# Side jobs at half the density in the pair stage, the time steps' sums among them; attention's units split before their value products; 1.4 instead of 1.5 pieces of filler a scan step

## The chip, the cores and the metric

The kernel runs on one core of one Trainium2 chip, as one launch. A core has a matrix engine (TensorE, PE in the profile; PEld are its weight loads), a vector engine (VectorE, DVE), an activation engine (ScalarE, ACT), a general engine (GpSimd, POOL), a queue engine that issues most transfers (SyncE, SP), and 16 DMA engines. Each engine works through its own list of instructions in order; semaphores let one wait for another. The metric is the device time in microseconds (us); lower is better.

## The reference

One layer of a streaming encoder on 1024 prompt tokens and 64 tokens of a running stream (1088 in all here), width 1024, all in float32:

```python
xn = _rmsnorm(x, p['norm_mix_w'])
proj = xn @ p['w_in']
z, xbc, dt_raw, q, k, v, gate_ssm, gate_att = jnp.split(proj, ...)
xbc_c = jax.nn.silu(causal_dwconv(conv_past, xbc))
dt = jax.nn.softplus(dt_raw + p['ssm_dt_bias'])      # the time steps
y_ssm, ssm_new = _ssd_scan(xs, dt, -exp(p['ssm_a_log']), bm, cm, ...)
q = _partial_rope(_rmsnorm(q, p['q_norm_w']), q_pos)
k = _partial_rope(_rmsnorm(k, p['k_norm_w']), q_pos)
o = _diff_attention(q, k_all, v_all, q_pos, k_pos, lam)
o = _rmsnorm(o, p['subln_w']) * (1.0 - lambda_init)
mix = sigmoid(gate_ssm) * (y_ssm @ w_branch_ssm) + sigmoid(gate_att) * (o @ w_branch_attn)
x = x + mix @ p['w_out']
x = x + ConvFFN(_rmsnorm(x, p['norm_ffn_w']))
```

Attention has 8 heads of two components each (the second's probabilities are subtracted, weighted), in blocks of 128 queries; the scan works on chunks with decays from running sums of dt times a constant per head.

## The kernel before

Each float32 operand is split into a high and a low part (`split`: ACT casts the high part, DVE subtracts), and a product is three matmuls of 128 x 128 weights with 272 columns (high-high, high-low, low-high). The stages, in order of time:

- **Values** (to about 152 us): `values(f, ...)` makes four groups of 256 columns of v, two of them with dt beside it. While `third` and `fourth` run, `rooted(k)` prepares the rows for the next stage on DVE and ACT, and after the tenth of their units `steps()` computes the time steps: some 20 vector instructions on 128 x 288, then sums over tokens on TensorE (L469, L472 and the nine of L482), whose results go to `nacum`, `decs`, `dtw` and to the scratch tensor `a_sc`, which the scan reads.
- **Pairs** (about 152 to 776 us): the projections q, k, z and the convolution inputs ("c"), 26 pairs of 2 x 128 columns, by a seven-product scheme. A pair is 14 groups (p, s) of 12 matmuls, in `pile` at L597; after each group ACT or DVE takes the result out of the bank (`u1`, `u2`, `pre`). The order of pairs is INPUT: 4 of q, 4 of k, 3 of z, then three times four of "c" and one of z. A "c" pair also has four convolutions of three vector instructions (L627). Beside the groups go side jobs, a generator `beside` advanced by `next(beside, None)`: `cached_keys`, `finishing("q")` and `finishing("k")`, which norm q and k, write k to the output and, at the end, rotate two of the eight row tiles in four parts (`turned`: L735 to L748). A side job loads in one part and works in the next (`in_turn`), and draws its row tiles from the rings "fx" (two) and "fc" (three), the latter shared with the convolutions.
- **Attention** (about 780 to 1244 us): per head nine blocks in ATT_ORDER. `attend` makes scores (L950, L951) and softmax, stops, and later does transposes (L979) and value products (L998); DEEP = 2 blocks lie between. When a head's last block is done, `head_out` norms its outputs (`o_t`, L1019 on DVE), transposes them (L1020) and stores them. Between blocks, `fill(ATT_STEPS)` issues pieces of a filler, projections of gates and z by `project` (L155 to L157, in 24 matmuls of 272 columns); a rate of 1 stands for 363 columns.
- **Scan** (about 1240 to 1690 us): 36 steps over chunks and groups with 12 turns between spans; at each of the 48 turns `fill(SCAN_STEPS)` issues filler, first what is left of the gates, then two of the three branch products. What remains is run behind the scan, and then the third branch product, which reads the scan's last rows back from DRAM (L205 casts them).
- **Output and feed-forward** (to the end).

The source order is not the order on the engines: a scheduler places every instruction on its engine's list by priority and by its own estimate of time. `tc.issue_after(x)` keeps what it encloses from being placed before instruction x; `seen[...]` holds the last instruction of a kind. `stat(w)` gives the one bank of its kind for small sums, `acc(w)` the next of seven banks.

Of the kernel before, what the change touches and what calls it, by code (L numbers as in the profile page):

```python
# [17 lines left out]
P = 128  # L18
# [50 lines left out]
SCAN_STEPS = 1.5  # L69
# [14 lines left out]
def hybrid_layer(ctx: ExitStack, tc: tile.TileContext, xT, xt, prm, cst, rope, wvd, win, wbs, wba, wout, wup, wdn,  # L84
# [360 lines left out]
    def steps():  # L445
        four = [raw_row(n) for n in ("da", "af")]
        da, e, t = (four[0][:, 288 * i : 288 * (i + 1)].rearrange("p (a b) -> p a b", b=32) for i in range(3))
        tail = raw_row("dt2")
        t2 = tail[:, :288].rearrange("p (a b) -> p a b", b=32)
        u = dtw  # L450
        act(e, u, AF.Abs)
        act(e, e, AF.Exp, scale=-1.0)
        V.tensor_scalar_add(t, e, 2.0)
        V.reciprocal(t, t)
        V.tensor_tensor(out=t, in0=t, in1=e, op=ALU.mult)
        V.tensor_tensor(out=t2, in0=t, in1=t, op=ALU.mult)
        V.tensor_scalar(e, t2, 1.0 / 17, None, ALU.mult)
        for n in (15, 13, 11, 9, 7, 5, 3):
            V.scalar_tensor_tensor(e, e, 1.0 / n, t2, ALU.add, ALU.mult)
        V.scalar_tensor_tensor(e, e, 1.0, t, ALU.add, ALU.mult)  # L460
        V.tensor_scalar_max(u, u, 0.0)
        V.scalar_tensor_tensor(dt_tok, e, 2.0, u, ALU.mult, ALU.add)
        an = tail[:, 288:320]
        act(an, par[:, O_AL : O_AL + 32], AF.Exp)
        V.scalar_tensor_tensor(da, dt_tok, -1.0, an.unsqueeze(1).to_broadcast([P, 9, 32]), ALU.mult, ALU.mult)
        V.memset(da[TS:, 8, :], 0.0)
        flat = lambda x: x.rearrange("p a b -> p (a b)")
        pa = acc(288)
        PE.matmul(pa, tri, flat(da), start=True, stop=True)  # L469
        V.tensor_scalar(flat(nacum), pa, -1.0, None, ALU.mult)  # L470
        pl = acc(288)
        PE.matmul(pl, ones, flat(da), start=True, stop=True)  # L472
        act(flat(decs), pl, AF.Exp)
        V.tensor_tensor(out=flat(dtw), in0=pl, in1=flat(nacum), op=ALU.add)
        act(dtw, dtw, AF.Exp)
        V.tensor_tensor(out=dtw, in0=dtw, in1=dt_tok, op=ALU.mult)
        af = four[1][:32]
        for c, w in WIDE:
            pf = acc(512)
            for i in range(c // P, -(-(c + w) // P)):  # L480
                n = min(P, T - i * P)
                PE.matmul(pf[:32, i * P - c : i * P - c + n], da[:n, i], tri[:n, :n], start=True, stop=True)  # L482
            V.tensor_copy(af[:, c : c + w], pf[:32, :w])
        load(out=a_sc[:8].rearrange("c h t -> h c t"), in_=af[:, :TP].rearrange("h (c t) -> h c t", t=P))
        load(out=a_sc[8, :, :TS], in_=af[:, TP:T])
# [98 lines left out]
    def in_pair(n):  # L584
# [5 lines left out]
        def pile(key, p, s, start):  # L590
# [3 lines left out]
            for k in range(4):  # L594
                c = slice(P * k, P * (k + 1))
                for i, (x, y) in enumerate(((0, 0), (0, 1), (1, 0))):
                    PE.matmul(ps, w[x][:, c], b[y][:, k], start=start and k == i == 0, stop=k == 3 and i == 2,  # L597
                              skip_group_check=not start)
# [84 lines left out]

    def in_turn(items):
# [12 lines left out]
    def finishing(kind):  # L697
# [6 lines left out]
        for c, w in WIDE:  # L704
            ps = stat(w)
            PE.matmul(ps, blk, rs[:, c : c + w], start=True, stop=True)
# [71 lines left out]

    early = [plain_left(0), plain_left(1)]
# [21 lines left out]
    for n in range(1, len(INPUT)):  # L801
        coming = in_parts(n + 1) if n + 1 < len(INPUT) else iter(())
        u = pairs[1] if n == 1 else begun_in(n)
        for at, (p, s) in enumerate(rest if n == 1 else [(p, s) for p in range(7) for s in range(2)]):
# [3 lines left out]
            if at % 2 == 0:  # L808
                next(beside, None)
# [62 lines left out]
    with (tc.tile_pool(name="ak", bufs=1) as ak, tc.tile_pool(name="at", bufs=1) as at,  # L872
# [209 lines left out]
        for f in late:  # L1082
            f()
# [704 lines left out]
```

## Time and profile before

| | |
|---|---|
| median of 3 runs | 2616.3 us (2616.27 to 2619.97) |
| the profiled execution | 2610.97 us; its span 2609.2 us |
| TensorE busy | 2419.7 us, 93% of the span, mean granted clock 0.968 |
| DVE, ACT, POOL busy | 1790.5, 1233.3, 738.4 us |
| TensorE busy, 400 to 500 us | 66.2 us of 100, granted clock 0.81 |
| TensorE busy, 800 to 1200 us | 86 to 92 us of 100, granted clock 0.90 to 0.93 |

A row of the waits names engine, tile and line, then the engine, tile and line that released it, the total, how often, and the longest. A row of stretches has the stretch, its length, then busy time and instructions of PE, PEld, DVE, ACT and POOL, the granted clock as a share of full speed, the mean busy share of the DMA engines, and GB/s. A row in order of time has start, length, engine, line, operation, output<-input, shapes and count, and in brackets the idle time before it with what ended it.

### The profile page before, as it was taken

How to read it: one execution, taken by the hardware profiler on the slowest of the kernel's cores; microseconds unless marked ns; L12 is line 12 of the kernel's file. 1: busy time of each engine (PE TensorE's matmuls, PEld its weight loads, DVE VectorE, ACT ScalarE, POOL GpSimd, SP SyncE). 2: the span in 40 equal slices, each digit the busy share in tenths (PEclk: the TensorE clock that was granted, in tenths of full speed). 3: DMA queues.
4: the chain of work that ended last, by engine and by line, in shares of the span. 5: the costliest groups of instructions: out<-in, count | busy, mean ns of one | idle time of the engine just before them, and what ended most of it. 6: DMA issues, size and time to landing. Idle time of an engine off the chain costs nothing.

```text
span 2609.2 us, 48402 instructions
## 1 busy us (share of the span) xinstructions
PE 2419.7 (93%) x18504; PEld 2324.4 (89%) x18504; DVE 1790.5 (69%) x3063; ACT 1233.3 (47%) x2613; POOL 738.4 (28%) x702
## 2 busy tenths in 40 slices
PE   9599998599998988889999999799999999998999
PEld 8599888599998878778878889799999999998999
DVE  4656776789885666664578766664897767778763
ACT  6244363345444555554576665433443333344441
POOL 0002223245420000000344433201245554545443
PEclk9799999799999988989999999999999999999999
DMA  7645657532246544532679785566323324348974
GB/s 247 216 159 191 226 164 249 168 113 101 101 138 205 159 144 142 163 114 75 221 267 307 264 292 171 158 188 208 114 87 109 143 75 178 114 157 253 228 200 88
DMA packets 282410, 449.72 MB, mean 172 GB/s; under 512 B 34937, under 2 KB 185602, under 8 KB 282178
## 3 DMA queue, kind: packets, MB, share of 16 engines
q1 hardware_dynamic: 274978, 433.54, 50.4%
q0 software_dynamic: 7200, 13.09, 3.2%
q8 instruction: 145, 2.38, 0.4%
q14 instruction: 87, 0.71, 0.1%
HBM read 294.03 MB, written 152.50 MB: 171 GB/s over the span
## 4 chain that ended last, share of the span: by engine, by line
PE 53%; DVE 10%; DMA 8%; ACT 5%; issue 3%; POOL 2%; SPq 1%; DVEq 0%; POOLq 0%; ACTq 0%
PE mx L1449 8%; PE mx L597 7%; PE mx L1607 4%; PE mm L155 4%; PE mm L157 4%; PE mm L156 4%; PE mm L1449 3%; PE po L998 3%; PE mm L597 3%; PE mm L1607 2%; PE mx L155 1%; PE mx L157 1%; PE mx L156 1%; PE sc L950 1%; DMA ht<-h_sc 1%
## 5 line engine op out<-in xcount | busy, mean ns | idle before, releaser
L155 PE MATMUL mm<-b,w_hi 128*128 128x272 f32 x1152 | 345.0, 300 | 18.9 <-ACT b L205 11.6
L157 PE MATMUL mm<-b,w_lo 128*128 128x272 f32 x1152 | 339.5, 295 | 2.6 <-DVE w_lo L149 2.4
L156 PE MATMUL mm<-b,w_hi 128*128 128x272 f32 x1152 | 339.9, 295 | 0.0
L155 PEld LDWEIGHTS mm<-b,w_hi 128*128 128x128 f32 x1152 | 220.8, 192 | 26.0 <-ACT b L205 13.3
L1128 POOL TENSOR_SCALAR_AFFINE_SELECT bc<-bc 128x1024 f32<-128x1024 f32 (+1 forms) x36 | 40.3, 1119 | 659.5 <-DMA start<-in_st_dram 506.1
L157 PEld LDWEIGHTS mm<-b,w_lo 128*128 128x128 f32 x1152 | 220.5, 191 | 6.4 <-DVE w_lo L149 4.5
L156 PEld LDWEIGHTS mm<-b,w_hi 128*128 128x128 f32 x1152 | 221.1, 192 | 4.2 <-issue 3.0
L405 DVE TENSOR_TENSOR wh<-w_f,wh 128x512 fp32r<-128x512 f32 (+1 forms) x174 | 173.6, 999 | 50.0 <-ACT wh L404 49.8
L524 POOL TENSOR_TENSOR ws<-w_f 128x512 f32<-128x512 f32 (+1 forms) x56 | 78.9, 1408 | 449.9 <-DMA q_r<-pre 186.6
L404 ACT CAST w_hi<-ws 128x512 fp32r<-128x512 f32 (+1 forms) x120 | 73.3, 611 | 170.0 <-PE mx L1449 74.6
L1449 PE MATMUL mx<-n,wh 128*128 128x272 f32 x1128 | 150.1, 288 | 1.9 <-ACT wh L404 1.1
L1449 PEld LDWEIGHTS mx<-n,wh 128*128 128x128 f32 x1128 | 144.5, 188 | 2.5 <-ACT wh L404 1.3
L1449 PE MATMUL mx<-m,w_hi 128*128 128x272 f32 x752 | 144.9, 290 | 1.2 <-DVE hb L1485 0.8
L964 ACT ACTIVATE p_t<-sc,mx 128x512 f32<-128x512 f32 (+5 forms) x144 | 106.2, 740 | 79.1 <-DVE mx L955 24.3
L597 PE MATMUL mx<-t,wh 128*128 128x272 f32 x936 | 129.8, 293 | 8.1 <-DVE u L668 8.1
L597 PE MATMUL mx<-t,w_hi 128*128 128x272 f32 x568 | 111.0, 291 | 24.0 <-ACT pre L677 24.0
L627 DVE SCALAR_TENSOR_TENSOR cc<-pre,par,cc 128x544 f32<-128x544 f32 (+1 forms) x144 | 131.4, 940 | 0.4
L597 PEld LDWEIGHTS mx<-t,wh 128*128 128x128 f32 x936 | 123.0, 191 | 9.7 <-DVE u L668 9.2
L404 ACT CAST wh<-w_f 128x512 fp32r<-128x512 f32 (+1 forms) x174 | 106.4, 615 | 49.5 <-issue 14.9
L597 PE MATMUL mx<-b,wh 128*128 128x272 f32 x864 | 118.6, 292 | 4.4 <-ACT u L666 4.4
L1466 POOL TENSOR_TENSOR hb<-hb,cc 128x544 f32<-128x544 f32 (+2 forms) x66 | 90.5, 1385 | 107.0 <-DVE hb L1487 49.4
L1449 PEld LDWEIGHTS mx<-m,w_hi 128*128 128x128 f32 x752 | 117.9, 188 | 2.5 <-DVE hb L1485 2.0
(445 smaller groups left out, 7408.1 us busy)
## 6 DMA issues: line engine op xcount, KB each, us to landing
w_f<-in_win_dram SPq DMA_DIRECT2D x78, 512.0 KB, 4.0
w_f<-in_wup_dram SPq DMA_DIRECT2D x45, 512.0 KB, 3.7
bc<-a_sc SPq DMA_DIRECT2D x32, 512.0 KB, 5.8
h_sc<-hb SPq DMA_DIRECT2D x44, 272.0 KB, 2.1
ht<-h_sc SPq DMA_DIRECT2D x22, 544.0 KB, 4.7
t_sc<-ht SPq DMA_DIRECT2D x22, 544.0 KB, 2.8
out_dram<-yq POOLq DMA_DIRECT2D x44, 272.0 KB, 6.0
g_sc<-gt SPq DMA_DIRECT2D x64, 136.0 KB, 2.4
```

The costliest lines, as they stand in the source:

```text
L155: PE.matmul(ps, a_hi, b_hi, start=i == 0, stop=False)
L156: PE.matmul(ps, a_hi, b_lo, start=False, stop=False)
L157: PE.matmul(ps, a_lo, b_hi, start=False, stop=i == n - 1)
L404: S.copy(hi, src)
L405: V.tensor_tensor(out=lo, in0=src, in1=hi, op=ALU.subtract)
L524: by.tensor_tensor(out=s1, in0=q21, in1=q22, op=ALU.add)
L597: PE.matmul(ps, w[x][:, c], b[y][:, k], start=start and k == i == 0, stop=k == 3 and i == 2, skip_group_check=not start)
L627: V.scalar_tensor_tensor(cc[:, :n], pre[:, i : i + n], cw(i), cc[:, :n], ALU.mult, ALU.add)
L964: act(p_t[:n, :nk], sc[c][:n, :nk], AF.Exp, bias=mx[:n, c : c + 1], accum_out=dst)
L1449: PE.matmul(ps, w[x][:, c], b[y][:, k], start=start and k == i == 0, stop=k == 3 and i == 2, skip_group_check=not start)
L1466: G.tensor_tensor(out=hb[h][:, o : o + n], in0=hb[h][:, o : o + n], in1=cc[:, d : d + n], op=ALU.mult)
L1607: PE.matmul(ps, w[y][:, c], b[z][:, k], start=start and k == j == 0, stop=k == n - 1 and j == 2, skip_group_check=not start)
```

## The change

Five edits:

1. `steps()` is a generator now, in eight parts, and runs as the first of the side jobs instead of between the value units. It draws its rows from the pair stage's rings and one tile of the ring "ss", its sums use `stat`, and `issue_after` puts them behind the latest product of the pair.
2. A side job's part comes after every fourth group instead of every second; `finishing("q")` and `finishing("k")` are both appended after the fourth pair, so that one follows the other. The sums within `finishing` are placed behind the latest product, too.
3. In attention, a unit stops a second time, between its transposes and its value products, and the filler is issued there instead of after the value products.
4. `head_out` is a generator: the nine scalings in its first part, one empty part, then its transposes in three parts, one part a block.
5. SCAN_STEPS is 1.4 instead of 1.5.

```diff
-SCAN_STEPS = 1.5
+SCAN_STEPS = 1.4
...
-    def steps():
-        four = [raw_row(n) for n in ("da", "af")]
...
-    for i, u in enumerate(chain(third, fourth)):
+    for u in chain(third, fourth):
         next(making, None)
-        if i == 9:
-            steps()
...
-                    PE.matmul(ps, w[x][:, c], b[y][:, k], ...)
+                    seen["mm"] = PE.matmul(ps, w[x][:, c], b[y][:, k], ...)
...
+    def steps():
+        flat = [four[:, 288 * i : 288 * (i + 1)] for i in range(3)] + [row("fx", "dt2")[:, :288]]
...
+        V.tensor_tensor(out=t2, in0=t, in1=t, op=ALU.mult)
+        yield
+        V.tensor_scalar(e, t2, 1.0 / 17, None, ALU.mult)
...
+        pa = stat(288)
+        with tc.issue_after(seen["mm"].ins):
+            PE.matmul(pa, tri, flat(da), start=True, stop=True)
+        V.tensor_scalar(flat(nacum), pa, -1.0, None, ALU.mult)
+        yield
...
+        for c, w in WIDE:
+            af = row("fc", "af")[:32, :w]
+            pf = stat(512)
...
+            yield
...
-    beside = cached_keys()
+    beside = chain(steps(), cached_keys())
...
-            if at % 2 == 0:
+            if at % 4 == 0:
                 next(beside, None)
...
-        if n in (3, 7):
-            beside = chain(beside, finishing("q" if n == 3 else "k"))
+        if n == 3:
+            beside = chain(beside, finishing("q"), finishing("k"))
...
                     V.tensor_copy(a4[:TS, :n], pt[:TS, :n])
+            yield
             po = pa.tile([P, 512], F32, name="po", tag="pt", bufs=2)
...
+            for i in range(9):
+                n = min(P, T - i * P)
+                V.scalar_tensor_tensor(o_t[:n, i], o_t[:n, i], rs[:n, i : i + 1], wsub[:n], ALU.mult, ALU.mult)
+            yield
+            yield
             for b0 in range(0, 9, 4):
...
-                    V.scalar_tensor_tensor(o_t[:n, i], o_t[:n, i], rs[:n, i : i + 1], wsub[:n], ALU.mult, ALU.mult)
                     PE.transpose(pt[:, (i - b0) * P : (i - b0) * P + n], o_t[:n, i], ident[:n, :n])
...
+                yield
...
                 unit, done = waiting.pop(0)
+                next(unit)
+                with tc.issue_after(seen["scores"].ins):
+                    fill(rate)
                 run(unit)
                 if done is not None:
-                    late.append(done)
+                    run(ended)
+                    ended = done()
...
-                while late:
-                    late.pop(0)()
+                next(ended, None)
...
-                settle(DEEP)
-                with tc.issue_after(seen["scores"].ins):
-                    fill(ATT_STEPS)
+                settle(DEEP, ATT_STEPS)
```

Where instructions stand now. First TensorE's list in the value stage, before: the steps' sums (L469, L472, L482; `da` is their operand) between two value units.

```order
L157 MATMUL mm<-b_906,xn_lo_102 128x256
L469 MATMUL mm<-da,con 128x288
L472 MATMUL mx<-da,con 128x288
L482 MATMUL mx<-con,da 32x128 x8
L482 MATMUL mx<-con,da 32x64
L155 MATMUL mx<-b_904,xn_hi_101 128x256
```

After, on TensorE in the pair stage (L553 are the products of a pair, L666 the first sum, whose operand lies in the tile `st`):

```order
L553 MATMUL mm<-b_1611,w_hi 128x272
L553 MATMUL mm<-b_1612,w_hi 128x272
L553 MATMUL mm<-b_1611,w_lo 128x272
L666 MATMUL st<-st,con 128x288
L553 MATMUL mm<-t_926,wh 128x272
```

The sums have moved from the value stage into the pair stage, between two groups, and the value units follow one another. Second, DVE's list where k is rotated, before (L741 to L748 are a rotation, L405 with `rt` its split; `rp` are cosines and sines):

```order
L741 SCALAR_TENSOR_TENSOR x<-x,par,ss 128x272 x2
L745 TENSOR_TENSOR rt<-x,rp 128x544
L741 SCALAR_TENSOR_TENSOR x<-x,par,ss 128x272 x2
L746 TENSOR_TENSOR x<-x,rp 128x544
L747 TENSOR_TENSOR x<-x,rt 128x272
L748 TENSOR_TENSOR x<-x,rt 128x272
L745 TENSOR_TENSOR rt<-x,rp 128x544
L746 TENSOR_TENSOR x<-x,rp 128x544
```

After, the same on DVE (L753 to L756 are L745 to L748 of before; L635 and L624 take a pair's results out of the banks, L583 is the convolution):

```order
L754 TENSOR_TENSOR x<-x,rp 128x544
L635 TENSOR_TENSOR pre<-mx,u_6318 128x272
L755 TENSOR_TENSOR x<-x,rt 128x272
L756 TENSOR_TENSOR x<-x,rt 128x272
L635 TENSOR_TENSOR pre<-mx,u_6318 128x272
L583 SCALAR_TENSOR_TENSOR cc<-pre,par,cc 128x547
L405 TENSOR_TENSOR w_lo<-ws_6356,w_hi 128x512
L405 TENSOR_TENSOR w_lo<-w_f,w_hi 128x512
L583 SCALAR_TENSOR_TENSOR cc<-pre,par,cc 128x547
L405 TENSOR_TENSOR x<-x,rt 128x544
```

Before, two rotations stood in each other, with nothing of a pair between; now the pair's own rows lie between a rotation's. Third, TensorE's list at the end of a head, before (L950 and L951 scores, L1020 the transposes of `head_out`, L979 those of a unit, L998 value products):

```order
L950 MATMUL sc<-kh_10044,q_10042 128x256
L951 MATMUL sc<-kl_10047,q_10042 128x256
L1020 MATMUL pt_10223<-con,o_t 128x128 x4
L1020 MATMUL pt_10238<-con,o_t 128x128 x4
L1020 MATMUL pt_10253<-con,o_t 128x64
L979 MATMUL pt<-con,p_t 128x128 x4
L950 MATMUL sc<-kh_10055,q_10061 128x512
```

After, around the second of the three pieces on TensorE (L1034 is L1020 of before, L988 is L979, L1008 is L998, L959 and L960 the scores; the first piece stands 35 rows earlier and the third 12 later):

```order
L959 MATMUL sc<-kh_9984,q_9982 128x128
L960 MATMUL sc<-kl_9987,q_9982 128x128
L1008 MATMUL po<-v_t,a_t 128x128
L1034 MATMUL pt_10356<-con,o_t 128x128 x4
L959 MATMUL sc<-kh_9995,q_10001 128x512
L960 MATMUL sc<-kl_9998,q_10001 128x512
L959 MATMUL sc<-kh_10004,q_10001 128x128
```

The nine transposes have been torn into three pieces with scores, value products and filler between them, and DVE's scalings for them stand ahead of the first.

More of the change, by code (lines that the diff above doesn't have):

```diff
@@ L705, in finishing @@
             ps = stat(w)
-            PE.matmul(ps, blk, rs[:, c : c + w], start=True, stop=True)
+            with tc.issue_after(seen["mm"].ins):
+                PE.matmul(ps, blk, rs[:, c : c + w], start=True, stop=True)
             t = [row("fx", "n1") for _ in range(2)]
@@ L777, in begun_in @@
         return u
+    four = row("ss", "st")
     early = [plain_left(0), plain_left(1)]
@@ L1026, in head_out @@
                     load(out=o_sc[D * u + P * h : D * u + P * (h + 1), b0 * P : b0 * P + w], in_=t.bitcast(F32))
+                yield
         fill(FIRST)
@@ L1081, in hybrid_layer @@
         settle(0)
-        for f in late:
-            f()
+        run(ended)
     with (tc.tile_pool(name="sin", bufs=1) as sin, tc.tile_pool(name="sp", bufs=1) as sp,
```

84 lines of the change are left out of this document (40 added, 44 removed).

## The prediction

> **What bounds the kernel now.** I read the engines' busy shares first, then TensorE's waits over the whole program, then tables of equal stretches of time, and then the order of time at each wait that the change touches.
>
> ```profile
> span 2609.2 us, 48402 instructions
> PE 2419.7 (93%) x18504; PEld 2324.4 (89%) x18504; DVE 1790.5 (69%) x3063; ACT 1233.3 (47%) x2613; POOL 738.4 (28%) x702
> ```
>
> TensorE is the bound, so time can only be won where it stands or runs slowly. Its longest waits (line waited at, releaser: total us, times, longest):
>
> ```profile
> PE mm L469 <- issue: 29.3, 1, 29.3
> PE mx L597 <- ACT pre L677: 24.0, 1, 24.0
> PE pt L1020 <- DVE o_t L1019: 11.4, 4, 5.3
> PE pt L1020 <- DVE ol L1024: 8.4, 7, 3.8
> PE pt L979 <- DVE ol L1024: 5.0, 6, 1.2
> PE mm L155 <- ACT b L205: 11.6, 1, 11.6
> ```
>
> Each belongs to one part of the change: the steps' sums (L469), the pair stage with its side jobs (L597), the end of a head in attention (L1020, L979), the end of the scan (L155, wait on L205). Waiting is not the whole loss, since the granted clock falls with it. I therefore count matmul records in equal stretches and compare with a full stretch (columns: stretch, length, busy us and records of PE, PEld, DVE, ACT, POOL, granted clock, DMA):
>
> ```profile
> 400.00:500.00 100.00, 66.20 (x461) 64.93 (x460) 67.06 (x112) 31.49 (x56) 20.50 (x26) 0.81 0.66 222
> 600.00:700.00 100.00, 100.00 (x794) 99.83 (x793) 87.06 (x133) 47.90 (x86) 45.26 (x58) 1.00 0.29 103
> 800.00:900.00 100.00, 92.35 (x637) 85.70 (x638) 69.46 (x165) 56.52 (x162) 0.00 (x0) 0.91 0.60 178
> 900.00:1000.00 100.00, 90.07 (x612) 80.67 (x612) 67.91 (x169) 54.88 (x159) 0.00 (x0) 0.93 0.49 149
> 1000.00:1100.00 100.00, 86.35 (x583) 77.33 (x581) 62.00 (x155) 52.97 (x153) 0.00 (x0) 0.90 0.45 140
> 1100.00:1200.00 100.00, 86.64 (x575) 77.41 (x573) 62.36 (x151) 52.02 (x146) 0.00 (x0) 0.90 0.34 108
> ```
>
> In the pair stage 794 records fill 100 us, so the stretch 400 to 500 did 58 us of work and lost 42, though PE was idle only 34 of it. A pair has 168 products, 21.2 us at that rate.
>
> **Term 1, the steps' sums leave the value stage.** TensorE reaches them before DVE has made their operand:
>
> ```profile
> 114.25 0.79 DVE L405 TENSOR_TENSOR t<-xt,t 128x272 fp32r<-128x272 f32 x2
> 123.76 1.30 PE L469 MATMUL mm<-da,con 128*128 128x288 f32 x2 [29.34 <-issue]
> 125.95 1.28 PE L482 MATMUL mx<-con,da 128*32 128x128 f32 x5
> 120.00:130.00 10.00, 6.24 (x29) 4.55 (x30) 6.20 (x15) 0.85 (x2) 0.00 (x0) 0.59 0.00 0
> 130.00:140.00 10.00, 10.00 (x87) 10.00 (x86) 0.00 (x0) 1.43 (x3) 0.00 (x0) 1.00 0.20 55
> 152.00 0.41 PE L597 MATMUL mm<-b,w_hi 128*128 128x272 f32 x2
> ```
>
> The wait is 29.3 us. Of the 6.2 us behind it, at granted clock 0.59, some 4.4 went to the sums themselves and to slow records. The sums return in the pair stage at full clock: about 4 us of records at half clock, so 2 us (estimate from the two rows). That is 29.3 + 4.4 - 2 = 31.7. The value products behind the wait then run while DVE still splits the rows for the pairs; its last split is at 114 to 115 us, and the pair stage would start near 152 - 32 = 120, so the next thing late has 5 us of room, less what the value stores now add to a full DMA queue. I take 30; bounds 24 (the room is gone and the first pair waits) and 34.
>
> **Term 2, side jobs at one part per four products.** From the second pair on, side jobs go at half the density. The start of a pair shows on DVE as the first use of L668; between these two lie ten pairs:
>
> ```profile
> 229.37 0.78 DVE L668 TENSOR_TENSOR u<-mx,u 128x272 f32<-128x272 f32 x2
> 451.30 0.78 DVE L668 TENSOR_TENSOR u<-mm,u 128x272 f32<-128x272 f32 x2
> 508.25 0.43 DVE L668 TENSOR_TENSOR u<-mm,u 128x272 f32<-128x272 f32 x1
> ```
>
> They took 278.9 us where 212 would do: 67 lost, 36 of them in the one pair from 451 to 508, in which the four rotations of k stand one behind the other in DVE's row. They wait for their own transfers, and the pair's evacuations stand behind them (DVE's waits in 300 to 560, and its groups in 466 to 494):
>
> ```profile
> DVE x L405 <- DMA out_dram<-x: 12.5, 8, 2.7
> DVE x L741 <- DMA x<-k_r: 9.0, 3, 5.5
> L741 DVE SCALAR_TENSOR_TENSOR x<-x,par,ss 128x272 f32<-128x272 f32 x8 | 3.7, 498 | 9.0 <-DMA x<-k_r 9.0
> L745 DVE TENSOR_TENSOR rt<-x,rp 128x544 f32<-128x544 f32 x4 | 2.9, 724 | 0.1
> ```
>
> In the new order a load has 6 us (four groups of 12 products, 1.5 us each) until its use instead of 3, against the 5.5 us of the longest wait, and the rotations are interleaved with evacuations. So most of the 67 goes. What comes late next is DVE. The side jobs now last until the nineteenth pair instead of the thirteenth, and from the twelfth on most pairs are convolution pairs (a convolution pair, then a gate pair):
>
> ```profile
> 602.40:623.60 21.20, 21.20 (x170) 21.14 (x169) 20.68 (x32) 10.65 (x20) 10.52 (x14) 1.00 0.31 104
> 666.00:687.20 21.20, 21.20 (x170) 21.20 (x170) 12.31 (x22) 8.13 (x15) 6.66 (x10) 1.00 0.29 104
> L405 DVE TENSOR_TENSOR x<-x,xh 128x544 fp32r<-128x544 f32 x8 | 8.6, 1080 | 3.2 <-DMA out_dram<-x 1.7 <-ACT xh L404 1.5
> L727 DVE SCALAR_TENSOR_TENSOR x<-x,wq,ss 128x544 f32<-128x544 f32 x7 | 6.0, 855 | 8.9 <-DMA x<-q_r 8.7
> ```
>
> DVE is at 20.7 of 21.2 there already. The nine pairs concerned hold 8 x 20.7 + 12.3 = 178 us of it; to that come k's twelve parts at 1.5 to 1.9 (the two rows, the lower end from two passes like L745) = 18 to 23, and six rotations (k's four, two of q's) at 4 us, an estimate from two of their six vector groups (3.7/4 and 2.9/4) = 24, against 191 us of TensorE: 29 to 34 over. Evacuation may lag by a few us (seven banks, 1.5 us each, so some 6), which leaves about 25; the pairs before the twelfth keep about a third of what nine pairs lose now beside the one of 57 us (31 us, 3.4 a pair), some 12. The steps' vector work, the 9 us between the first two rows of term 1 and some 2 behind them, goes to three pairs of the kind that leaves DVE a third free (67 of 100 in the row at 400), and is hidden there; were it not, it would cost those 11. So 67 - 25 - 12 = 30, and I take 27, since DMA waits of 1 to 2 us per k part cannot be hidden where DVE is full. Bounds: 55 if DVE keeps pace and only the lighter pairs' 12 stay; -10 if evacuation may not lag (34), both transfer waits of the list (21.5) come back where DVE is full, the lighter pairs keep 12 and POOL beside it adds another 10.
>
> The Trainium skill, page "GPSIMD Engine Reference", section "1. Specifications", says that GpSimd shares its SBUF interfaces with VectorE and contends with vector instructions that have two SBUF inputs. This speaks against the move: nearly all side-job work has two such inputs, and by the rule its 45 us would cost half as much again beside a POOL that is half busy, so the term would be near 5 rather than 27. The trace agrees in part: the split L405 took 1080 ns in the mean over 294 to 400, the two-input pass L745 of the same size 724 over 466 to 494.
>
> **Term 3, attention.** A full quarter of 100 us next to the end of a head, as it is now:
>
> ```profile
> 875.00:900.00 25.00, 24.71 (x185) 22.91 (x184) 18.81 (x43) 14.34 (x46) 0.00 (x0) 1.00 0.66 196
> 1017.73 2.31 PE L1020 MATMUL pt<-con,o_t 128*128 128x128 f32 x8 [4.11 <-DVE o_t L1019]
> 1016.00:1018.00 2.00, 0.27 (x2) 0.19 (x2) 1.93 (x7) 0.39 (x2) 0.00 (x0) 0.50 0.00 0
> 1028.00:1030.00 2.00, 2.00 (x14) 2.00 (x13) 0.00 (x0) 0.08 (x1) 0.00 (x0) 0.65 0.00 0
> 861.12 0.39 PE L950 MATMUL sc<-kh,q 128*128 128x256 f32 x1 [1.76 <-ACT p_t L964]
> 863.00:865.00 2.00, 2.00 (x8) 1.50 (x7) 1.71 (x5) 0.23 (x2) 0.00 (x0) 0.50 1.00 371
> ```
>
> At 185 records per 25 us, the 2407 records of 800 to 1200 are 325 us of work, so 75 are lost, about 9 at each of the eight head ends: the transposes stand in front of DVE's nine scalings, then the clock is 0.50 for some 13 us. In the new order the scalings are two units ahead of the first transposes, and the transposes come in three pieces with scores and filler between. That removes the waits on L1019 and L1024 (24.8 us in the list) and most of the slow clock. What is late next is DVE again, 18.8 of 25 in a full stretch and 1.9 of 2 in the row at 1016, at a head's end, and the chain through ACT within the scalings' part. The row at 861 shows a wait of 1.8 us that still brought the clock to 0.50. I take two thirds of the loss, 50; bounds 75 (all of it) and 20 (the waits shift to the scores).
>
> The Trainium skill, page "TensorE: Matmul & The Clock Gate", section "Part 1: The HAM clock gate", states that the clock drops only after an idle window of about 3.4 us and returns after about as much activity. By it the waits that stay, all shorter, would cost no clock and the term would be 70 or more; the row at 861 disagrees, and I follow the row.
>
> **Term 4, 1.4 pieces a scan step.** 48 turns take 4.8 pieces less (of 363 columns, 24 products of 272 columns being 3.0 us: some 19 us), which run behind the scan instead. There TensorE waits for the last rows to be normed, stored and read again:
>
> ```profile
> 1680.00:1700.00 20.00, 7.93 (x48) 7.49 (x46) 8.78 (x22) 9.17 (x19) 0.00 (x0) 0.74 0.52 159
> 1700.00:1720.00 20.00, 17.86 (x128) 16.53 (x129) 13.22 (x31) 8.21 (x19) 0.00 (x0) 1.00 0.63 196
> 1720.00:1740.00 20.00, 20.00 (x161) 20.00 (x160) 13.99 (x31) 7.49 (x16) 0.00 (x0) 1.00 0.63 192
> ```
>
> At 161 per 20 us the first two lost 18 us. The new order has eight products of 24 behind the last scan step, instead of one, ahead of the waiting ones: enough. I take 17; bounds 20, and 5 if the scan's steps are not as short as their TensorE work and keep their old length.
>
> **The sum.** 30 + 27 + 50 + 17 = 124. The profiled execution took 2610.97 us (span 2609.2 and 1.8 around it), 5.3 under the median 2616.3, so 2487 by it and 2492 against the median. All bounds at once give 2616 - 184 = 2432 and 2616 - 39 = 2577.
>
> **Rivals.** (a) DVE overload in the convolution pairs eats term 2: it is 0 to -10, total 2519 to 2529. For it: DVE at 20.7 of 21.2; against it: the interleaving. Chance 0.16. (b) Attention's wait only moves, from the transposes to the scores behind DVE: term 3 is 20, total 2522. For it: the 1.76 us row; against it: 18.8 of 25 between the ends. Chance 0.13. (c) Short waits cost no clock (the skill's gate): term 3 is 72, total 2470. Chance 0.13. (d) Slower: the ring "fc" of three row tiles serves the convolution and the side jobs; if side jobs in convolution pairs hold it, each such pair goes like that from 451 to 508, 36 us over. Six of the eight such pairs would cost 216, and with the old 67 gone and 97 gained elsewhere that is 52 slower, 2668; it decides from about five. Against it: the one such pair now had its four rotations in a row, and the new order has none so. Chance 0.03. (e) The edits cancel, within 0.2% (5 us, what a measurement here can tell from no change): 0.02. My forecast, all terms near their values, has 0.53 and a range of its own of 2465 to 2515.
>
> **How the numbers follow.** 2492 is the likeliest. The range 2448 to 2552 takes in (a), (b) and (c) with some mixing, and leaves out (d), (e) and the far ends. Faster by over 0.2%: 0.95; within: 0.02; slower: 0.03.
>
> **What would show it.** Right: no wait of TensorE on the sums' operand, and the first product of the pair stage near 120 us; ten pairs near 230 us with no pair of 57; in attention no wait on the scalings and records near 170 per 25 us at the head ends; full stretches behind the scan. Wrong: pairs of 25 us and more with DVE full between the twelfth and the nineteenth; a clock of 0.50 once per head still; TensorE waiting on filler weights late in the scan.

## The result: 105 us faster, 19 less than predicted

The changed kernel takes 2511.3 us (median of 4 runs, 2506.2 to 2512.1) beside 2616.3 us for the kernel before on the same chip: a ratio of 0.9597, 95% interval 0.9574 to 0.9621. The prediction was 2492, range 2448 to 2552. The head of the profile after:

```profile
span 2509.5 us, 48443 instructions
PE 2390.5 (95%) x18504; PEld 2302.9 (92%) x18504; DVE 1782.3 (71%) x3063; ACT 1231.0 (49%) x2615; POOL 720.0 (29%) x702
```

The work is the same; TensorE is busy 29 us less, since more of it runs at full clock, and stands 71 us less. Its longest waits now:

```profile
PE sc L959 <- ACT p_t L973: 25.9, 20, 8.1
PE mx L553 <- DVE u L624: 10.3, 6, 3.3
PE mx L553 <- DVE pre L635: 9.3, 8, 2.9
PE po L1008 <- DVE a_t L995: 8.6, 7, 2.7
PE mx L553 <- ACT u L622: 6.7, 2, 4.9
```

The waits of the first list of before are gone or under 1 us: on the steps' sums (29.3 us), on `pre` from ACT (24.0), on the scalings (11.4), on `ol` at a head's end (13.4), on `b` behind the scan (11.6). Largest now are the scores that wait for an exponential to free their bank (L959) and the pair products that wait for DVE to empty theirs (L624, L635). The stages begin at these rows (first pair product, first score), and the two stretches behind them are the pair stage and attention, before and after:

```profile
117.36 0.41 PE L553 MATMUL mx<-b,w_hi 128*128 128x272 f32 x2
729.35 0.40 PE L959 MATMUL sc<-kh,q 128*128 128x512 f32 x1
```

```profile
152.00:782.45 630.45, 576.58 (x4430) 569.90 (x4429) 488.27 (x785) 291.92 (x517) 198.02 (x216) 0.96 0.49 165
782.45:1240.40 457.95, 409.39 (x2814) 372.08 (x2813) 280.71 (x684) 237.65 (x679) 0.00 (x0) 0.92 0.47 144
```

```profile
117.36:729.35 611.99, 575.58 (x4452) 566.36 (x4451) 495.47 (x809) 293.58 (x522) 190.85 (x216) 0.99 0.51 171
729.35:1153.88 424.53, 386.12 (x2815) 355.25 (x2814) 275.37 (x684) 235.75 (x680) 0.00 (x0) 0.98 0.51 155
```

By the same marks (the scan ends where the feed-forward part makes its first product) the 99.7 us between the two spans divide into 34.6 of the value stage, 18.5 of the pairs, 33.4 of attention, 17.3 of the scan, less 4.1 in the rest, whose code is the same. The table gives these stages for every kernel run below, from its profiled execution, with the median of its runs:

| kernel | median | values | pairs | attention | scan, output | rest |
|---|---|---|---|---|---|---|
| before | 2616.3 | 152.0 | 630.5 | 458.0 | 641.9 | 726.9 |
| after | 2511.3 | 117.4 | 612.0 | 424.5 | 624.5 | 731.1 |
| u1 steps back | 2523.7 | 151.0 | 590.1 | 422.7 | 625.8 | 728.1 |
| t1 dense for the steps | 2503.8 | 118.0 | 597.1 | 425.3 | 627.6 | 733.3 |
| u2 dense throughout | 2537.6 | 117.2 | 636.9 | 427.9 | 624.7 | 730.2 |
| p3 three densities | 2502.5 | 116.9 | 599.6 | 430.3 | 626.9 | 728.0 |
| m1 no POOL sums | 2485.4 | 117.0 | 583.4 | 429.1 | 625.6 | 728.5 |
| u3 old attention | 2547.7 | 116.2 | 609.5 | 458.1 | 634.2 | 729.6 |
| a1 filler behind | 2505.0 | 117.2 | 607.3 | 417.4 | 629.9 | 731.8 |
| h1 head's end in one piece | 2516.9 | 117.3 | 603.7 | 432.2 | 628.9 | 729.1 |
| a3 more filler | 2513.3 | 117.0 | 607.5 | 459.1 | 603.6 | 723.5 |
| u4 1.5 pieces | 2534.9 | 116.9 | 606.9 | 428.5 | 645.2 | 730.5 |
| c1 p3 and a1 | 2501.3 | 116.7 | 602.5 | 418.6 | 629.0 | 727.9 |
| c2 p3, first blocks filled | 2499.1 | 117.3 | 601.4 | 421.5 | 629.1 | 727.8 |

How far such a number can be trusted is seen where the code is the same: the pairs as in after take 607 to 612 us (after, u3, a1, a3, u4), attention as in after 423 to 430. Differences of under 6 us between two stages are not read. After lies at the long end of the first and near the short end of the second: by the means of these kernels the pairs as changed take 608.6 us and attention 426.9. Some shorter stretches repeat more closely: the three pairs behind the opening one take 59 to 61 us in the eleven kernels that have both the steps' sums and POOL's sums in the pair stage.

Inside the pair stage both halves of the prediction's second term stand. Before, the ten pairs from the fourth and the twelve behind them, and the same after:

```profile
229.37:508.25 278.88, 232.07 (x1716) 227.24 (x1715) 196.63 (x327) 121.03 (x216) 72.11 (x63) 0.92 0.58 196
508.25:760.43 252.18, 249.31 (x1969) 248.25 (x1968) 224.79 (x350) 123.62 (x220) 113.85 (x146) 1.00 0.31 104
```

```profile
199.26:429.66 230.40, 221.94 (x1733) 219.00 (x1731) 171.04 (x284) 112.84 (x204) 64.77 (x63) 1.00 0.53 179
429.66:707.31 277.65, 256.00 (x1980) 251.94 (x1981) 249.03 (x399) 135.90 (x240) 111.68 (x143) 0.99 0.49 163
```

The ten pairs gained 48.5 us, and the twelve lost 25.5 of them again, with DVE busy 249 of 278 us and 10.6 of its idle 29 spent on k's loads. The slowest pair now, and a light one for comparison:

```profile
550.12:583.65 33.53, 26.82 (x195) 25.95 (x194) 30.76 (x48) 12.53 (x23) 18.14 (x19) 0.95 0.48 151
220.49:241.44 20.95, 20.95 (x168) 20.95 (x168) 12.70 (x24) 9.92 (x19) 3.77 (x3) 1.00 0.72 232
```

### The profile page after: what moved, and what is told of

Same layout as the page of the kernel before. It is cut to its first block, busy times and chain, and to the rows that moved or that the text cites. A ratio compares the mean times of both kernels' runs of the same rounds, so it can differ in the third digit from the quotient of the medians.

```text
span 2509.5 us, 48443 instructions
## 1 busy us (share of the span) xinstructions
PE 2390.5 (95%) x18504; PEld 2302.9 (92%) x18504; DVE 1782.3 (71%) x3063; ACT 1231.0 (49%) x2615; POOL 720.0 (29%) x702
## 4 chain that ended last, share of the span: by engine, by line
PE 62%; DVE 13%; DMA 11%; ACT 6%; issue 4%; POOL 2%; SPq 1%; DVEq 0%; POOLq 0%; ACTq 0%
PE mx L553 9%; PE mx L1464 8%; PE mx L1622 5%; PE mm L155 5%; PE mm L157 5%; PE mm L156 5%; PE mm L553 4%; PE mm L1464 3%; PE mx L155 2%; PE po L1008 2%; PE mm L1622 2%; PE mx L157 2%; PE mx L156 2%; DMA ht<-h_sc 2%; DVE cc L583 1%
## 5 line engine op out<-in xcount | busy, mean ns | idle before, releaser
L405 DVE TENSOR_TENSOR wh<-w_f,wh 128x512 fp32r<-128x512 f32 (+1 forms) x174 | 163.3, 939 | 46.5 <-ACT wh L404 46.1
L583 DVE SCALAR_TENSOR_TENSOR cc<-pre,par,cc 128x544 f32<-128x544 f32 (+1 forms) x144 | 131.9, 937 | 0.3 <-ACT cc L581 0.2
L553 PE MATMUL mx<-t,wh 128*128 128x272 f32 x840 | 116.0, 291 | 11.6 <-DVE u L624 10.3
L553 PE MATMUL mx<-t,w_hi 128*128 128x272 f32 x608 | 118.5, 291 | 3.6 <-DVE pre L635 3.6
L553 PEld LDWEIGHTS mx<-t,wh 128*128 128x128 f32 x840 | 109.5, 189 | 13.5 <-DVE u L624 11.6
L553 PE MATMUL mx<-b,wh 128*128 128x272 f32 x840 | 115.6, 290 | 2.3 <-ACT u L622 1.7
```

Of the source, the lines that this page charges most:

```text
L405: V.tensor_tensor(out=lo, in0=src, in1=hi, op=ALU.subtract)
L553: seen["mm"] = PE.matmul(ps, w[x][:, c], b[y][:, k], start=start and k == i == 0, stop=k == 3 and i == 2, skip_group_check=not start)
L583: V.scalar_tensor_tensor(cc[:, :n], pre[:, i : i + n], cw(i), cc[:, :n], ALU.mult, ALU.add)
```

## The experiments

**The steps' sums put back (u1).** `steps()` stands in the value stage as before; the rest is as changed.

```diff
-    for u in chain(third, fourth):
+    for i, u in enumerate(chain(third, fourth)):
         next(making, None)
+        if i == 9:
+            steps()
...
-    beside = chain(steps(), cached_keys())
+    beside = cached_keys()
```

> The changed kernel with the steps' sums back in the value stage, in one piece after the tenth unit; all else as changed (the side jobs have eight parts fewer and so end two pairs earlier). Theory, each edit pays in its own stage: TensorE waits some 29 us for the sums' operand again, the pair stage begins at 150 to 153 us instead of 117; the first pair loses its 4 us of waiting again in return, so the time is 2511 + 30 = 2541 (2536 to 2546). Rival, the move only shifted the loss into the pair stage: the pair stage is shorter by 15 us and more, total at most 2530.

Measured: 2523.7 us, only 12 above after. The wait in the value stage came back in full, but the pair stage became 22 us shorter:

```profile
PE mm L469 <- issue: 29.7, 1, 29.7
151.02:741.17 590.15, 569.70 (x4430) 562.77 (x4429) 487.62 (x785) 290.21 (x515) 197.90 (x216) 0.99 0.53 176
```

The rival holds: beside the thinner side jobs the steps' sums cost the pair stage more than half of what the value stage gains (18.5 us of some 34, when the mean of 608.6 is taken for the pairs as changed). Four places share the 22 us: the opening pair, 4 (18.3 for 21.9; it takes 17.2 to 19.4 in kernels with the code of after, so this is the one execution); the three pairs behind it, 5 (55.0 for 60.0); the ten, 6 (224.4 for 230.4; 226.4 to 230.4 in the five kernels with the pairs of after); the late twelve, 7 (270.5 for 277.7; 277.1 to 278.9 in those five).

**What they cost there (t1).** The side jobs' first parts go at the old density again, for four pairs.

```diff
-            if at % 4 == 0:
+            if at % (2 if n < 4 else 4) == 0:
```

> The changed kernel with a part after every second group in the first four pairs only, where the steps' sums and the cached keys are; then after every fourth, as changed. The side jobs of q begin where they begin without the steps' sums among them (at the fifth pair). Theory, the 22 us that the pair stage lost to the steps' sums (612 with them, 590 without) are not their own instructions but q's and k's parts pushed two pairs back, into convolution pairs: the pair stage takes 596 to 601, the time is 2497 to 2503. Rival, it is their own work on DVE and TensorE: the pair stage stays at 607 to 614, the time within 5 us of 2511.

Measured: pair stage 597.1, as the theory had it; time 2503.8, 1 us above its range. The ten pairs take 224.1 us and the twelve 271.6, as in u1: some 12 of the 22 us were the pushing back of q's and k's parts. The stretch behind the opening pair stays long. From there to the fourth pair, in u1 and in t1:

```profile
169.30:224.32 55.02, 55.02 (x439) 55.02 (x438) 43.95 (x75) 24.59 (x46) 11.65 (x8) 1.00 0.61 207
```

```profile
137.59:197.30 59.71, 58.36 (x451) 56.36 (x450) 52.23 (x92) 23.36 (x46) 13.63 (x10) 1.00 0.45 149
```

DVE works 8 us more there, TensorE 3 more. These 5 us are the work of the steps itself and not the density, since after, with the thinner side jobs, takes 60.0 us there too.

**The old density throughout (u2).**

```diff
-            if at % 4 == 0:
+            if at % 2 == 0:
...
-        if n == 3:
-            beside = chain(beside, finishing("q"), finishing("k"))
+        if n in (3, 7):
+            beside = chain(beside, finishing("q" if n == 3 else "k"))
```

> The changed kernel with a side job's part after every second group again, and k's finishing appended after the eighth pair, as before; all else as changed (so the eight parts of the steps' sums are among the side jobs). Theory, term 2 as the traces give it: the ten pairs from the fourth to the fourteenth take some 280 us instead of 230, the twelve behind them 252 instead of 278, so 23 us are lost, 2534 (2528 to 2542). Rival, what made the late pairs slow is not the side jobs in them but DVE beside POOL's weight sums: the late twelve stay at 270 and more, and the total is 2555 and more.

Measured: 2537.6 us, 26 above after; the ten pairs take 283.0, the late twelve 254.1. So term 2 is worth 25 with the steps' sums in the pair stage. From before to u1, without them there, it is 40 (630.5 to 590.1). The same edit has two prices, by whether the other has been made.

**Three densities (p3).** Every second group to the fourth pair, every third to the eleventh, then every fourth.

```diff
-            if at % 4 == 0:
+            if at % (2 if n < 4 else 3 if n < 11 else 4) == 0:
```

> The changed kernel with the side jobs after every second group in the first four pairs, after every third up to the eleventh, then after every fourth: they end some three pairs earlier, before the sixteenth pair instead of in the nineteenth. Theory, what the late pairs lose is DVE's work of the side jobs in convolution pairs, so fewer such pairs lose less: the late twelve pairs take 265 us instead of 278, the ten before them 235 instead of 230 (a load has 4.5 us until its use), the pair stage 604, the time 2503 (2496 to 2509). Rival, the waits of the denser parts on their loads cost as much again: 2515 and more.

Measured: 2502.5 us, pair stage 599.6. The side jobs end three pairs earlier; the late twelve take 266.8, the ten 232.9, both about 2 us from the expectation. What the late pairs lose is the side jobs' share in them. But every third group up to the eleventh pair brought nothing beyond t1, which has only the first four pairs dense: 597.1 us there, 599.6 here, since the ten pairs lose (224.1 to 232.9) what the twelve gain (271.6 to 266.8).

**POOL's sums left out (m1, one run).** Is it DVE's own work, or POOL beside it?

```diff
-        return left_parts(blocks_of(n), early, V if n < 2 else G)
+        return left_parts(blocks_of(n), early, V if n < 2 else None)
```

With None, `s1`, `s2` and `q21` are blocks of the weights, and no sum is made.

> Leaves out part of the computation: POOL's sums of weight blocks in the pair stage (from the third pair on); blocks of the weights stand in for the sums, so the products have other values but the same shapes and number. Theory, DVE is slowed by POOL's work beside it: the convolution's rows L583 fall from 965 ns to about 700 and the splits from 960 to about 700, so that DVE has room in the convolution pairs; the late twelve pairs take at most 260 us instead of 278, the pair stage at most 590. Rival, DVE's own work is too much there: its rows keep their lengths within 5%, the pair stage is within 6 us of 612.

Three of DVE's groups in the convolution pairs, after (374 to 608 us), and without POOL's sums (374 to 590; L586 and L738 there are L583 and L735 of after):

```profile
L583 DVE SCALAR_TENSOR_TENSOR cc<-pre,par,cc 128x544 f32<-128x544 f32 x47 | 44.9, 965 | 0.0
L405 DVE TENSOR_TENSOR x<-x,xh 128x544 fp32r<-128x544 f32 x12 | 11.5, 960 | 0.0
L735 DVE SCALAR_TENSOR_TENSOR x<-x,par,ss 128x544 f32<-128x544 f32 x12 | 9.8, 814 | 10.6 <-DMA x<-k_r 10.6
```

```profile
L586 DVE SCALAR_TENSOR_TENSOR cc<-pre,par,cc 128x544 f32<-128x544 f32 x47 | 36.2, 778 | 0.1
L405 DVE TENSOR_TENSOR x<-x,xh 128x544 fp32r<-128x544 f32 x12 | 8.6, 720 | 1.6 <-DMA out_dram<-x 1.6
L738 DVE SCALAR_TENSOR_TENSOR x<-x,par,ss 128x544 f32<-128x544 f32 x12 | 9.4, 783 | 11.5 <-DMA x<-k_r 11.3
```

The convolution's rows fall by 19% and the splits by 25%, to 778 and 720 ns where 700 were expected, and the pair stage by 29 us to 583.4: POOL does slow DVE. But the late twelve pairs still take 266.2 us instead of the 260 expected, with DVE busy 214 of them. What is left there is not settled; 11 us of it are DVE's waits on k's loads, behind which the pair's evacuations stand. Leaving the sums out also takes away the waits on the sums themselves (in after ACT waits 16.7 us on them in the late twelve pairs), and 17 of the 29 us were gained before the late pairs, so the 29 us are an upper bound for the slowing by POOL.

**Attention as before (u3).** `head_out`, `settle` and the place of the filler are those of before.

> The changed kernel with attention as before: scalings and transposes of a head's end in one piece, filler behind the value products; all else as changed. Theory, the edit's gain is its stage's difference: attention takes 458 us instead of 424, the time is 2511 + 33 = 2544 (2539 to 2550). Rival, part of that difference came from attention starting with other loads done: the difference is 20 or less, 2531.

Measured: 2547.7, 36 above after; attention 458.1, as in before to 0.2 us. In attention the edits stand by themselves. They also reach into the scan: its stage takes 634.2 us here, 9.7 more than in after, with the same code and the same 1.4 pieces. TensorE waits 3.4 us once in the middle of it, with a clock of 0.83 over the 20 us around, and 5.1 us instead of 2.9 on weights of the filler at its end.

**Filler behind the value products, the head's end in parts (a1).**

```diff
-            yield
             po = pa.tile([P, 512], F32, name="po", tag="pt", bufs=2)
...
                 unit, done = waiting.pop(0)
-                next(unit)
-                with tc.issue_after(seen["scores"].ins):
-                    fill(rate)
                 run(unit)
...
-                settle(DEEP, ATT_STEPS)
+                settle(DEEP)
+                with tc.issue_after(seen["scores"].ins):
+                    fill(ATT_STEPS)
```

> The changed kernel with attention's filler behind the value products again, the head's end still in parts. Theory, the gain of attention (424 us instead of 458) comes from the head's end alone, where the waits on the scalings stood: attention takes at most 432 us and the time is 2511 to 2521. Rival, it is the filler between transposes and value products that covers the copies of the transposes: attention takes 445 and more, the time 2532 and more.

Measured: 2505.0, attention 417.4, both shorter than after, and the time below the 2511 to 2521 of the theory. A head's length is read from one end to the next (the scalings, L1026). In after the ends of the first and the seventh head are

```profile
810.80 2.44 DVE L1026 SCALAR_TENSOR_TENSOR o_t<-o_t,ors,wsub 128x128 f32<-128x128 f32 x9
1098.89 2.44 DVE L1026 SCALAR_TENSOR_TENSOR o_t<-o_t,ors,wsub 128x128 f32<-128x128 f32 x9
```

so the second to seventh heads take 288 us together; in a1 it is 288 as well, in before 326; the first takes 74.2 in a1, 74.0 in before and 81.4 in after. The third edit is worth nothing between the heads, and it costs 7 us at the start, because `settle` fills only when more than two blocks wait: the first two blocks have no filler.

**The first two blocks filled (c2).** The order of the change, the three densities, and:

```diff
+                if len(waiting) <= DEEP:
+                    with tc.issue_after(seen["scores"].ins):
+                        fill(ATT_STEPS)
                 settle(DEEP, ATT_STEPS)
```

> The three densities, with the filler ahead of the value products as changed, and filler also issued behind the first two blocks of attention, where the change issues none. Theory, the changed order of filler and value products is worth nothing by itself, and its only effect is the first head without filler in its first two blocks: the first head takes 74 to 75 us instead of 81 to 83, heads two to seven together 288 us as in both other orders, the time equals that of the kernel with the filler behind, 2496 (2491 to 2501). Rival, the first head is slow because the filler stands in front of its value products: 80 us and more, 2503.

Measured: 2499.1 us, ratio to before 0.9548, interval 0.9531 to 0.9565, wholly below that of after. The first head takes 77.2, which is between the two expectations (p3, the same kernel without this fill: 83.5); heads two to seven 289. So most, not all, of the 7 us were the missing filler; the share is rough, since the first head takes 78.7 to 83.5 us in the seven kernels with the attention of after.

**The head's end in one piece again, two blocks later (h1).** On c1, which joins p3 and a1:

```diff
                     load(out=o_sc[D * u + P * h : D * u + P * (h + 1), b0 * P : b0 * P + w], in_=t.bitcast(F32))
-                yield
+            yield
```

> The kernel with the three densities and the filler behind the value products (2501), in which the nine transposes of a head's end follow one another again, in one part, two blocks behind their scalings. Theory, what a head's end won (heads two to seven 288 us together instead of 326) is that the scalings are done long before the transposes; tearing the transposes apart adds little: 288 to 296 us, time 2500 to 2509. Rival, the transposes must be torn apart, since in one piece they wait for DVE's lower parts `ol` to free their two banks, as the waits of before show (13.4 us), and the clock falls with it: 304 us and more, time 2517 and more.

Measured: 2516.9; heads two to seven 299.5 us, between the two. Scalings two blocks ahead bring some 26 of the 38 us, tearing the transposes apart the other 12: in one piece they wait again for the banks, as these rows of h1 (the first two) and c1 (the third, all that it has of this kind) show:

```profile
PE pt L988 <- DVE ol L1037: 6.3, 4, 2.2
PE pt L1033 <- DVE ol L1037: 2.6, 3, 1.1
```

```profile
PE pt L988 <- DVE ol L1037: 0.9, 2, 0.7
```

**More filler in attention, less in the scan (a3).** `ATT_STEPS` 0.6 for 0.45, `SCAN_STEPS` 1.2 for 1.4.

> The changed kernel with 0.6 pieces of filler a block in attention instead of 0.45, and 1.2 a scan step instead of 1.4: some 10 pieces of 4 us of TensorE's work move from the scan into attention. Theory, attention's blocks are as long as the chain from scores over maximum and exponential to the transposes, not as TensorE's work, since the heads with more filler took no longer (45.6 us with 138 matmuls of it, 49.2 with 121): attention stays within 12 us of 424, the scan gets 30 to 38 us shorter, the time is 2480 to 2495. Rival 1, TensorE is the bound in attention too and the wait is due to its order: attention 455 to 465, the time within 8 us of 2511. Rival 2, the scan cannot get shorter, its own vector work and transfers being the bound there: attention as in the theory, scan within 12 us of before, time 2500 to 2515.

```profile
724.47:1183.56 459.09, 429.63 (x3162) 401.80 (x3161) 282.72 (x688) 246.70 (x698) 0.00 (x0) 0.98 0.50 153
```

Measured: 2513.3, attention 34.6 us longer. My theory fell, rival 1 holds: 347 more records took 34.6 us, where the pair stage's rate of 7.94 a us gives 43.7. About 9 us of attention were free for filler (15, if it is compared with the longest attention of the same code, 430), no more. The scan gave up the same 347 records and became only 21 us shorter, so it is not bound by TensorE alone either.

**1.5 pieces a scan step (u4).**

> The changed kernel with 1.5 pieces of filler a scan step instead of 1.4. Theory, 1.4 pays by covering the end of the scan: behind the scan TensorE waits again for the last rows, 13 to 18 us, 2526 (2522 to 2531). Rival, the changed attention leaves other amounts of filler, so that at 1.5 the end is covered too: within 5 us of 2511.

Measured: 2534.9, 23.5 above after and above the 2531 that the theory allowed; 18.4 between the profiled executions, 20.6 in the scan's stage alone. Behind the scan TensorE stands as it did before, the second row at a clock of 0.74:

```profile
1580.00:1600.00 20.00, 18.00 (x137) 17.18 (x135) 10.77 (x19) 13.26 (x24) 5.31 (x3) 1.00 0.74 229
1600.00:1620.00 20.00, 13.00 (x72) 12.16 (x72) 12.60 (x32) 7.61 (x21) 0.00 (x0) 0.74 0.65 188
```

In after the same place (the last row norm of the scan starts at 1563.5) reads:

```profile
1560.00:1580.00 20.00, 16.65 (x123) 15.96 (x122) 10.59 (x22) 12.10 (x27) 1.04 (x1) 0.95 0.58 171
1580.00:1600.00 20.00, 20.00 (x145) 20.00 (x144) 13.35 (x33) 10.37 (x26) 0.00 (x0) 0.88 0.85 252
```

**Two places put together (c1).**

> Two places put together: the three densities of the side jobs (pair stage 599.6 instead of 612), and the filler behind the value products again (the first head 74.2 instead of 81.4 us, the others as they were). Theory, both hold and do not touch each other: 2511 - 9 - 6 = 2496 (2491 to 2501). Rival, the fewer products left behind the scan cost what the first head gains: 2502.

Measured: 2501.3 us (5 runs, 2496.5 to 2504.4), 1 us below p3 alone. That is nearer to the rival's 2502, but the theory's range ends at 2501, so the time does not separate them. Attention keeps its gain (418.6), but the scan's stage takes 629.0 instead of 624.5 to 627.6, as in a1 (629.9), c2 (629.1) and h1 (628.9). At the end of the scan TensorE waits 5.1 to 5.7 us on weights of the filler in these four and in u3, and 2.8 to 3.0 us in after and the five kernels with its attention and its 1.4 pieces. The rows of c1 and of after:

```profile
PE mm L155 <- ACT w_hi L148: 5.2, 1, 5.2
```

```profile
PE mm L155 <- ACT w_hi L148: 2.9, 1, 2.9
```

Why these weights come later is not shown. It is not the filler spent in attention alone: a1, c1 and c2 spend 18 records more there than after (2833 for 2815), but h1 and u3 do not (2814). The intervals of c2 and c1 (0.9542 to 0.9573) are the ones that lie wholly below that of after; the two cannot be told from each other.

## Why the prediction came out

**Term 1 (30 forecast).** The mechanism and the mark were right: no wait on the sums, first pair product at 117.4 (near 120). The value stage gained 34.6. The opening pair took 21.9 us to the first use of L624 instead of 17.7, with a wait of 4.9 us on ACT, which makes 30.4; the other executions of the same code show that most of that wait belongs to this one. That it comes to 30 is in part luck, then. What I counted as hidden was not: the steps' own work costs the first pairs 5 us (I had counted 2, and 13 were it not hidden at all). I had read "a third free" from the row at 400, but TensorE did only 58 us of work in those 100 us; in u1, without the steps, DVE is busy 44 of the 55 us of these pairs, a fifth free. And the eight parts push all later side jobs back by up to two pairs, some 12 us (t1). Term 2 has them in its "until the nineteenth pair", but no step charged them to the move. So the move alone, made last, is worth 12 by the medians.

**Term 2 (27 forecast).** 48.5 gained in the ten pairs and 25.5 lost in the twelve: 23. The forecast was a lag of 25 there with DVE as the bound, and 12 kept in the lighter pairs (18.4 by the same count, 230.4 less 212). The pairs of 25 us and more, named as a sign of error, did come (five of them), at the price that the sum had put down. That this agrees to a microsecond is partly luck: DVE was not full but idle for 29 of the 278 us, 10.6 of them on k's loads, for which the sum had 3, and POOL slows DVE's rows there by up to a quarter (m1), which the sum had only in its lower bound. Terms 1 and 2 share the lag: counted as the change makes them, 57 were forecast and 53 came; split, they are 28 + 25 or 12 + 40, as the one or the other is made first (u2, u1).

**Term 3 (50 forecast): the mis-sized term.** 33.4 came. The step that failed is the count of 75 us of loss, of which I took two thirds as if what was removed would not come back. The waits on L1019 and L1024 went from 24.8 us nearly to zero and the clock rose from 0.92 to 0.98. But TensorE stood 48.6 us of attention before and still 38.4 after, only 10 less. What came back is above all the wait of the scores on the exponential, which was in before

```profile
PE sc L950 <- ACT p_t L964: 12.8, 11, 6.0
```

and is 25.9 us in after: 13 of the 17 us that are missing. In u3, with attention as before, it is 13.4. The other 23 of the 33 us are TensorE's shorter busy time.

The measure did not hold, either. By the same count, 7.4 records a us, 44 us would still be lost in after (2815 records in 424.5 us), and a3 could fill only 9 to 15 of them; attention as a whole ran at 6.6 records a us there and at 6.9 in a3, and no run reached the rate of the full quarter. Besides, the moved filler brought nothing and cost the first head 7 us, a cost that no step of mine had: I did not see that `settle` no longer fills behind the first two blocks. Without that the term would be 40. This overlaps with the scores' wait, which is 19.8 us in a1, without the moved filler.

Rival (b) is partly true, then: the wait moved to the scores, though the profile names ACT and not DVE as what ended it. Rival (c) as well: of TensorE's ten waits of 1.1 to 2.7 us in attention after, eight leave the clock at 1.00, but the time that it was to bring did not come. Rival (a) had the lag right and its price too high, and (d) did not come.

**Term 4 (17 forecast).** 17.3 in the profiles, 18 to 23 when undone. The mechanism is shown by u4. That the size fits is in part luck, since this edit, too, has two prices: with attention as before (u3) the scan's stage takes 634.2, so that 1.4 pieces alone bring 7.7 of the 17.3 and attention's edits the rest. The sign of error that I had named, TensorE waiting on filler weights late in the scan, is there with 2.9 us.

**The sum.** 30.4 + 23 + 33.4 + 17.3 = 104, less 4 us in the rest of the program, whose stage takes 723 to 733 us in kernels with the same code there. By the profiled executions that is 24 short of 124: 17 in term 3 and 4 each in term 2 and the rest of the program, while terms 1 and 4 brought 1 more than forecast. By the medians 19 are missing, since before's profiled execution lay 5 us under its median.

## What to carry to other kernels

Price edits in the order in which they are made, and count what a moved job pushes back in the queue that it joins: here eight short parts moved two pairs of later work into pairs whose vector engine was full, and with their own work ate about half of a 34 us gain. When a loop's filler is moved behind a condition, ask what the first rounds get. And a rate read from one full stretch is no floor for a stage whose stretches differ in kind: give the stage more filler, and see how much of it is free.

## What the runs showed of the hardware

The length of a wait alone does not decide what the clock does. In after, TensorE's wait of 2.36 us at 1095.7 left the granted clock at 1.00, and one of 1.94 us at 858.0 brought it to 0.50 for between 3 and 4 us:

```profile
858.00:860.00 2.00, 0.08 (x1) 0.08 (x1) 1.35 (x5) 1.99 (x8) 0.00 (x0) 1.00 0.06 20
860.00:862.00 2.00, 2.00 (x11) 1.91 (x12) 2.00 (x12) 0.78 (x4) 0.00 (x0) 0.75 0.00 0
862.00:864.00 2.00, 2.00 (x11) 2.00 (x10) 1.30 (x6) 0.00 (x0) 0.00 (x0) 0.50 0.00 0
1096.00:1098.00 2.00, 0.00 (x0) 0.00 (x0) 0.80 (x2) 1.99 (x7) 0.00 (x0) 1.00 0.02 4
1098.00:1100.00 2.00, 1.95 (x13) 1.85 (x14) 1.97 (x10) 1.84 (x7) 0.00 (x0) 1.00 0.00 0
```

A DVE instruction beside one of POOL can take more than three times as long. In order of time in after, a rotation's row beside a sum of POOL, and the same row without such a sum:

```profile
550.61 1.44 POOL L480 TENSOR_TENSOR ws<-w_f 128x512 f32<-128x512 f32 x1 [4.50 <-ACT cc L581]
550.82 1.53 DVE L756 TENSOR_TENSOR x<-x,rt 128x272 f32<-128x272 f32 x1
573.10 0.44 DVE L756 TENSOR_TENSOR x<-x,rt 128x272 f32<-128x272 f32 x1
```

The slow row ends 0.30 us behind the sum. p3 has another, at 455.97, which also takes 1.53 us and also ends 0.30 us behind the sum beside it. The row of 573.10 has only a short copy of POOL beside it; the others of L756 in these two kernels take 0.43 to 0.44 us.

The Trainium skill, page "GPSIMD Engine Reference", section "1. Specifications", has this contention for vector instructions with two SBUF inputs; here the trace agrees, with 1.53 us against 0.44.
